# A chunked recurrence with full-array chunk steps in a written order on the tensor engine, and its triangular solve taken half a sequence at a time

## The chip, the cores and the metric

The kernel runs on one core of a Trainium2 chip. The metric is the device time of one execution in microseconds (us); lower is better. A core has a tensor engine (PE, with its weight loads shown apart as PEld), a vector engine (DVE), a scalar engine (ACT), GpSimd (POOL) and a sync engine (SP), which here issues the DMAs. Each engine runs its own instructions strictly in order, and waits for others by semaphores. TensorE has two clock levels, 1.2 and 2.4 GHz; a granted clock of 1.00 is the upper one.

## What is computed

One decoder block over 1024 tokens of width 1024: a combined projection, a gated unit (SGU) on half of the channels, a linear recurrence (RWKV7, 8 heads of 64 x 64 state) on the other half, an output projection, and cross-attention over 256 memory tokens. Everything is f32. Cut to the part that the change touches:

```python
def rwkv7_step(state, inp):
    r, w, k, v, a, bb = inp
    sa = jnp.einsum('bhvk,bhk->bhv', state, a)
    state = state * w[:, :, None, :] + sa[..., None] * bb[:, :, None, :] + v[..., None] * k[:, :, None, :]
    y = jnp.einsum('bhvk,bhk->bhv', state, r)
    return state, y
...
h  = x + W_out [ SGU_group(z_A) ; RWKV7_group(z_B) ],   z = RMSNorm(x) @ W_in
h  = h + MemXAttn(RMSNorm(h), RMSNorm(mem))
```

## The kernel before

**Big products.** A projection is made of "dense" products, 128x512 outputs with 128x128 weights. For f32 accuracy each is three fp32r products of high and low parts: `mm3` (L174 to L176). They carry most of the work, and in the recurrence they are interleaved with it so that TensorE has something to do while a chunk's chain runs through other engines.

**The recurrence.** Heads go in 4 pairs, a pair's 1024 tokens in 2 halves of 512 (8 halves in all), a half in 2 quarters, a quarter in 4 chunks of 64 tokens. For each half:

- `elementwise` (first product at L558) makes decays and the scaled operands `ra` (r and a) and `bk` (b and k).
- `grams` (L631) makes the chunks' inner products, masks them on DVE (L636, L638, L639, L641), writes the 16x16 diagonal blocks to DRAM (L640), reads them back with one block per partition (L647), inverts them there in 14 dependent steps on DVE (L648, then L652 and L654 in turn), writes the inverses (L655) and reads them back as `t16` (four DMAs, L659).
- `turn` (L670, L676) transposes v and bk on TensorE.
- `solve` extends the 16x16 inverses to 64x64, in groups of 8 small products (L690), each waiting for DVE's or ACT's work on the one before; the first group reads `t16`.
- `serial` is the chain over chunks. In each, both heads of the pair are done by small products side by side in the array (64x64 or 128x64 parts of it): `us0` = state times a (L751), DVE adds it to `akv` (L752), `us1` = the solve's matrix `tt` times that (L754), ACT and DVE each copy one head to `avt` (L756, L757), `us2` = bk times avt (L760), DVE makes the new state (L764), and ACT copies it into a block-diagonal 128x128 tile `stdiag` (L767, five of them in turn). Every two chunks `outputs` forms y from `stdiag` (L731) and `avt` (L735), and ACT copies it out (L737).
- `finish` normalises y on DVE and ACT and writes it to DRAM.

**The order.** The loop at the end runs over 19 quarter steps. In each, `weave` interleaves the generators of several pipeline stages (serial of this quarter, solve of the next, grams one half ahead, elementwise further ahead) with 16 dense units of a projection tile (`z_fill`), or later with `out_proj`. A scheduler then still moves instructions within an engine's order; `behind` ties each solve group to the last `us1`. Stretches named here by "first chunk product" are cut at a half's first L754.

## Time and profile before

| | |
|---|---|
| time, median of 3 runs | 966.76 us (965.78 to 968.97) |
| the profiled execution | 965.16 us, its span 963.3 us |
| busy in the span | PE 936.3 us (97%), PEld 723.7 us (75%), DVE 576.1 us (60%), ACT 410.2 us (43%), POOL 50.2 us (5%) |
| recurrence region on PE | 248.67 us (first L558) to 697.37 us (first product of the next stage) |

Busy shares of TensorE count a product from its issue to its modelled end; products overlap in the pipeline, so the step from one start to the next is what a product takes of the engine. All times below are from the span's start.

### The profile page before, as it was taken

To read this page: it belongs to the slowest core of one execution; us is meant where nothing else is said; L and a number is where in the kernel's file an instruction comes from. 1 tells how busy PE (TensorE), PEld (TensorE's weight loads), DVE (VectorE), ACT (ScalarE), POOL (GpSimd) and SP (SyncE) were. 2 spreads that over 40 slices of the span, in tenths; PEclk is the share of its full clock that TensorE was granted. 3 is DMA by queue.
4 is the path that set the end of the run, shared out by engine and by line. 5 is a ranking of instruction groups with operands and counts; after the bars stand their busy time and mean duration, and the time that the engine had idled before them with its cause. 6 is when DMAs were issued, how large, how long until landed. Compare 5 with 4: busy or idle time off the path is not lost.

```text
span 963.3 us, 17125 instructions
## 1 busy us (share of the span) xinstructions
PE 936.3 (97%) x6724; PEld 723.7 (75%) x6724; DVE 576.1 (60%) x1343; ACT 410.2 (43%) x918; POOL 50.2 (5%) x110
## 2 busy tenths in 40 slices
PE   6999999999999999999999999999999999999997
PEld 5978888888776667666666666666788778888885
DVE  5867234344575786767676787765677654444333
ACT  6764122224433545353535372534356643333222
POOL 0001000010100000000000000000000000000000
PEclk9999999999999999999999999999999999999999
DMA  8762011122112111111111172333472300000011
GB/s 316 252 224 97 12 69 67 66 95 81 40 49 48 34 30 38 38 45 37 48 37 48 37 242 80 99 92 97 130 248 70 127 23 1 22 22 22 22 43 46
DMA packets 86097, 76.93 MB, mean 80 GB/s; under 512 B 38272, under 2 KB 58752, under 8 KB 86016
## 3 DMA queue, kind: packets, MB, share of 16 engines
q1 hardware_dynamic: 84864, 73.73, 24.6%
q10 hardware_dynamic: 1152, 2.10, 0.6%
q8 instruction: 53, 0.87, 0.4%
q14 instruction: 28, 0.23, 0.1%
HBM read 62.17 MB, written 13.64 MB: 79 GB/s over the span
## 4 chain that ended last, share of the span: by engine, by line
PE 86%; DVE 5%; DMA 3%; issue 2%; ACT 2%; POOL 1%; SPq 0%; POOLq 0%; DVEq 0%; ACTq 0%
PE mm L174 23%; PE mm L175 22%; PE mm L176 21%; PE cb L690 5%; PE us L754 2%; PE yps L731 2%; PE us L760 2%; PE us L751 1%; PE co L631 1%; PE yps L735 1%; PE co L676 1%; DMA xr<-in_xT 1%; DMA w_raw<-in_w_sv 1%; DMA pr<-in_w_qT 1%; PE co L429 1%
## 5 line engine op out<-in xcount | busy, mean ns | idle before, releaser
L174 PE MATMUL mm<-xh,w_hi 128*128 128x512 f32 x400 | 167.3, 418 | 0.0
L175 PE MATMUL mm<-xl,w_hi 128*128 128x512 f32 x400 | 161.0, 402 | 0.0
L176 PE MATMUL mm<-xh,w_lo 128*128 128x512 f32 x400 | 159.9, 400 | 0.0
L154 DVE TENSOR_TENSOR w_lo<-w_raw,w_hi 128x512 fp32r<-128x512 f32 x115 | 78.7, 686 | 65.7 <-ACT w_hi L153 63.4
L153 ACT CAST w_hi<-w_raw 128x512 fp32r<-128x512 f32 x115 | 71.1, 619 | 97.8 <-PE mm L175 89.9
L174 PEld LDWEIGHTS mm<-xh,w_hi 128*128 128x128 f32 x400 | 75.3, 188 | 18.6 <-issue 2.4
L176 PEld LDWEIGHTS mm<-xh,w_lo 128*128 128x128 f32 x400 | 75.1, 188 | 15.5 <-issue 0.8
L175 PEld LDWEIGHTS mm<-xl,w_hi 128*128 128x128 f32 x400 | 75.2, 188 | 15.0 <-issue 2.1
L174 PE MATMUL mm<-wo,w_hi 128*128 128x512 f32 x128 | 53.4, 417 | 0.2 <-DVE kp_l L921 0.2
L175 PE MATMUL mm<-wo,w_hi 128*128 128x512 f32 x128 | 53.1, 415 | 0.0
L176 PE MATMUL mm<-wo,w_lo 128*128 128x512 f32 x128 | 52.8, 413 | 0.1
L174 PE MATMUL mm<-vp_h,p_hi 128*128 128x512 f32 x128 | 51.3, 401 | 0.0
L767 ACT COPY stdiag<-state 64x64 f32<-64x64 f32 x120 | 29.1, 243 | 50.3 <-DVE state L764 42.0
L174 PE MATMUL mm<-kp_h,w_hi 128*128 128x512 f32 x128 | 50.1, 391 | 0.0
L176 PE MATMUL mm<-kp_h,w_lo 128*128 128x512 f32 x128 | 50.0, 391 | 0.0
L176 PE MATMUL mm<-vp_h,p_lo 128*128 128x512 f32 x128 | 50.0, 390 | 0.0
L175 PE MATMUL mm<-vp_l,p_hi 128*128 128x512 f32 x128 | 49.9, 390 | 0.0
L175 PE MATMUL mm<-kp_l,w_hi 128*128 128x512 f32 x128 | 49.9, 390 | 0.0
L989 DVE TENSOR_REDUCE mx<-mm 128x2 f32<-128x512 f32 x16 | 11.1, 691 | 41.7 <-PE mm L176 41.7
L495 ACT ACTIVATE t<-mm,vec 128x512 f32<-128x512 f32 x34 | 23.3, 684 | 21.5 <-PE mm L176 21.4
L756 ACT COPY avt<-us 64x64 f32<-64x64 f32 x64 | 13.1, 205 | 44.7 <-PE us L754 44.1
L757 DVE COPY avt<-us 64x64 f32<-64x64 f32 x64 | 14.5, 226 | 29.0 <-ACT avt L756 27.5
(271 smaller groups left out, 2068.0 us busy)
## 6 DMA issues: line engine op xcount, KB each, us to landing
w_raw<-in_w_blk SPq DMA_DIRECT2D x50, 256.0 KB, 2.7
w_raw<-y_scr SPq DMA_DIRECT2D x32, 256.0 KB, 3.0
w_raw<-in_w_kv SPq DMA_DIRECT2D x17, 256.0 KB, 4.0
xr<-in_xT SPq DMA_DIRECT2D x8, 512.0 KB, 5.7
w_raw<-in_w_out SPq DMA_DIRECT2D x16, 256.0 KB, 2.6
h_all<-in_x SPq DMA_DIRECT2D x16, 256.0 KB, 4.2
pr<-in_w_qT SPq DMA_DIRECT2D x8, 512.0 KB, 4.2
w_raw<-in_w_o SPq DMA_DIRECT2D x16, 256.0 KB, 2.7
```

The lines of the kernel that those rows point to most:

```text
L153: nc.scalar.copy(out=hi, in_=src)
L154: (eng or nc.vector).tensor_tensor(out=lo, in0=src, in1=hi.bitcast(F32), op=ALU.subtract)
L174: nc.tensor.matmul(ps, lh, rh, start=first, stop=False)
L175: nc.tensor.matmul(ps, lh, rl, start=False, stop=False)
L176: nc.tensor.matmul(ps, ll, rh, start=False, stop=last)
L495: nc.scalar.activation(out=t1[:, 1:HT + 1], in_=ps, func=AF.Copy, scale=vc("mu", b))
L690: nc.tensor.matmul(ps[R[hh], c, :], fl(hh, c), fr(hh, c), start=True, stop=True)
L731: nc.tensor.matmul(yps[R[j], 0:P], ra[:, c0 + c - 1 + j, 0, :], st_d[(i - 1 + j) % NST], start=True, stop=False, skip_group_check=True)
L754: mm = nc.tensor.matmul(us[R[hh], 1, :], tt[R[hh], c, :], akv[R[hh], c, :], start=True, stop=True)
L757: nc.vector.tensor_copy(out=avt[0:64, c, R[1]], in_=us[R[1], 1, :])
L760: nc.tensor.matmul(us[R[hh], 2, :], bkt[:, c, R[hh]], avt[:, c, R[hh]], start=True, stop=True)
L767: D_COPY(nc)(out=st_d[(i + 1) % NST][R[hh], R[hh]], in_=s_new[R[hh]])
```

## The change

The chunk step is done with three products over the full 128x128 array: `us0` (now L755) multiplies r and a at once with the block-diagonal state, so that its upper half is already the state's part of y, and two DVE additions (L757) put its lower half into a second block-diagonal tile `abdiag`, while ACT copies the y part out (L759); `us1` is L765 with one ACT copy to `avt` (L766); `us2` is L769, from which two DVE operations (L775) write the block-diagonal state itself. So the state's copies (L767) and L731 fall away. The other part of y (L787) is made once in a quarter and added on DVE (L789). `us` has one PSUM tile for its three parts. The solve takes a half at a time, four waits in place of five per quarter, 16 products to a group (L708; the third makes two groups at once), so `t16` is one tile whose four DMAs (L675) all belong to the first group. The loop runs over 10 steps of a half with 32 dense units in a full one (`z_stream`, which fetches its next weights ahead), and TensorE's order is the order of the program, with no scheduler (`manual_schedule`). The stages of a half keep their distance: grams and solve one half ahead of serial, elementwise two. The projection tile that stood third before the loop is now the first one in it.

```diff
 LOGA = math.exp(-0.5)
 SHIFT = 19.4
 W_RAW = 3
-NST = 5
-Y_LAG = 2
 QC = 4
 NRA = 3
-W_G = (0.0, 0.4)
-W_T = (0.263, 0.465)
-N_T16 = 3
-W_E = (0.2, 0.964)
-W_S = (0.337, 0.95)
-G3 = 10
-N_PROJ = 11
+W_Y1 = (0.0, 0.03)
+W_G = (0.01, 0.18)
+W_T0 = (0.28, 0.40)
+W_Y0 = (0.55, 0.57)
+W_T1 = (0.58, 0.68)
+W_S = (0.64, 1.0)
+W_E = (0.30, 0.98)
+W_F = (0.08, 0.36)
 W_C = (0.0, 1.0)
-W_F = (0, 0.836)
-N_END = 1
-D_COPY = lambda nc: nc.scalar.copy
+N_PROJ = (14, 28, 28)
 W_HL = 3
 N_KV = (11, 14)
-AF_S = True
-AF_Y = False
...
-        st_t = [rw.tile([P, C], F32, name=f"state{i}") for i in range(2)]
-        st_d = [rw.tile([P, P], F32, name=f"stdiag{i}") for i in range(NST)]
-        for t in st_d:
+        st_d = [rw.tile([P, P], F32, name=f"stdiag{i}") for i in range(2)]
+        ab_d = [rw.tile([P, P], F32, name=f"abdiag{i}") for i in range(2)]
+        for t in st_d + ab_d:
...
+        def z_stream(blocks, then):
+
+            num = lambda pw: 9 + 4 * pw[0] + pw[1]
+            nxt = load_blk(w_blk[num(blocks[0])])
+            for n, pw in enumerate(blocks):
+                cur, nxt, raws = nxt, [], []
+                for h in range(2):
+                    ps = mm_ps()
+                    ts = slice(h * HT, (h + 1) * HT)
+                    for kk in range(KT):
+                        hi, lo = cur[kk // 4]
+                        mm3(ps, hi[:, kk % 4, :], lo[:, kk % 4, :], xh[kk][:, ts], xl[kk][:, ts], kk == 0, kk == 7)
+                        i = 8 * h + kk
+                        if n + 1 < len(blocks):
+                            if i in (1, 2):
+                                raws.append(fetch(w_blk[num(blocks[n + 1])][:, 4 * i - 4:4 * i, :], [P, 4, P]))
+                            if i in (8, 12):
+                                nxt.append(halves(raws[len(nxt)], [P, 4, P]))
+                        elif i == 12:
+                            next(then)
+                        if kk < 7:
+                            yield
+                    z_evac(*pw)(h, ps)
+                    yield
...
-        def behind(on):
-
-            return tc.issue_after(state["last"]) if on and state["last"] is not None else nullcontext()
...
+            u["t16"] = t16 = rw.tile([P, NC, C], F32, name="t16")
             for j in range(2):
-                quarters[2 * i + j]["t16"] = t16 = rw.tile([P, QC, C], F32, name="t16", bufs=N_T16)
                 for hh in range(2):
-                    nc.sync.dma_start(out=t16[R[hh]], in_=ti[j, hh, :, 0:C, :].rearrange("c s t -> s c t"))
+                    nc.sync.dma_start(out=t16[R[hh], QC * j:QC * j + QC, :],
+                                      in_=ti[j, hh, :, 0:C, :].rearrange("c s t -> s c t"))
             yield
 
...
+        def solve(i):
+
+            u, qs = halves_u[i], quarters[2 * i:2 * i + 2]
+            t16 = u["t16"]
+            of = lambda key, hh, c, rows: qs[c // QC][key][hh][rows, c % QC, :]
+
+            def pair_mm(ps, fl, fr):
+                ps = ps.rearrange("p (c t) -> p c t", c=NC)
+                for c in range(NC):
+                    for hh in range(2):
+                        nc.tensor.matmul(ps[R[hh], c, :], fl(hh, c), fr(hh, c), start=True, stop=True)
                 return ps
 
...
+            ps = pair_mm(cb_ps(), lambda hh, c: of("ntl", hh, c, R[hh]), lambda hh, c: t16[R[hh], c, :])
...
+            pa = pair_mm(co_ps(), lambda hh, c: of("akl", hh, c, R[1]), lambda hh, c: qs[c // QC]["avt"][R[1], c % QC, R[hh]])
...
+        def serial(i):
+
+            u = halves_u[i]
+            ra, dc, tt, akv = u["ra"], u["dc"], u["tt"], u["akv"]
+            u["y"] = ytok = rw.tile([P, 4, P], F32, name="ytok", bufs=2)
+            for c in range(NC):
+                q = quarters[2 * i + c // QC]
+                avt, bkt, cq = q["avt"], q["bkt"], c % QC
+                first = i % 2 == 0 and c == 0
+                last = i % 2 == 1 and c == NC - 1
+                n = state["i"]
+                state["i"] += 1
+                dcc = dc[:, c:c + 1]
+                s_old, s_new, ab = st_d[n % 2], st_d[(n + 1) % 2], ab_d[n % 2]
+                us = psC.tile([P, 3, P], F32, name="us")
+                yc = ytok[R[c % 2], c // 2, :]
+                if first:
+                    nc.gpsimd.memset(yc, 0.0)
+                    for hh in range(2):
+                        nc.vector.tensor_copy(out=ab[R[hh], R[hh]], in_=akv[R[hh], c, :])
+                else:
+
+                    nc.tensor.matmul(us[:, 0, :], ra[:, c, :, :], s_old, start=True, stop=True)
+                    for hh in range(2):
+                        nc.vector.tensor_tensor(out=ab[R[hh], R[hh]], in0=us[R[1], 0, R[hh]], in1=akv[R[hh], c, :],
+                                                op=ALU.add)
+                    nc.scalar.copy(out=yc, in_=us[R[0], 0, :])
+                    if not last:
+                        sd = rw.tile([P, P], F32, name="sd")
+                        nc.scalar.activation(out=sd, in_=s_old, func=AF.Copy, scale=dcc)
+                yield
+
+                nc.tensor.matmul(us[:, 1, :], tt[:, c - c % 2:c - c % 2 + 2, :], ab, start=True, stop=True)
+                nc.scalar.copy(out=avt[R[0], cq, :], in_=us[R[c % 2], 1, :])
+                yield
+                if not last:
+                    nc.tensor.matmul(us[:, 2, :], bkt[:, cq, :], avt[:, cq, :], start=True, stop=True)
+                    for h2 in R:
+                        if first:
+                            nc.vector.tensor_scalar(out=s_new[h2, h2], in0=us[h2, 2, h2], scalar1=dcc[h2],
+                                                    scalar2=None, op0=ALU.mult)
+                        else:
+                            nc.vector.scalar_tensor_tensor(out=s_new[h2, h2], in0=us[h2, 2, h2], scalar=dcc[h2],
+                                                           in1=sd[h2, h2], op0=ALU.mult, op1=ALU.add)
+                yield
+
+        def outputs(n):
...
+            gr, avt = q["gr"], q["avt"]
+            yps = psC.tile([P, 512], F32, name="yps")
             for c in range(QC):
                 for hh in range(2):
+                    o = P * (c // 2) + 64 * hh
+                    nc.tensor.matmul(yps[R[c % 2], o:o + 64], gr[:, c, hh, :], avt[:, c, R[hh]], start=True, stop=True)
+            yt = u["y"][:, 2 * (n % 2):2 * (n % 2) + 2, :]
+            nc.vector.tensor_tensor(out=yt, in0=yt, in1=yps[:, 0:256].rearrange("p (c v) -> p c v", c=2), op=ALU.add)
...
+        for w in range(2):
+            z_block(9 + w, z_evac(0, w))
         proj = out_proj(steps_0, ahead)
-        for n in range(-3, NQ):
-            ok = lambda m: 0 <= m < NQ
-            e_now = ok(n + 3) and (n + 3) % 2 == 0
-            streams = [(grams((n + 2) // 2) if ok(n + 2) and n % 2 == 0 else iter(()), 5, *W_G),
-                       (turn(n + 2) if ok(n + 2) else iter(()), 2, *W_T),
-                       (elementwise(halves_u[(n + 3) // 2]) if e_now else iter(()), 7, *W_E),
-                       (solve(n + 1) if ok(n + 1) else iter(()), 5, *W_S),
-                       (serial(n) if ok(n) else iter(()), 5, *W_C),
-                       (finish(halves_u[n // 2 - 1]) if n > 0 and n % 2 == 0 else iter(()), 3, *W_F)]
-            if n in fills:
-                fill = z_fill(*fills[n])
-                weave(streams + [(fill, 16, 0.0, 1.0)])
+        blocks = [(0, 2), (1, 0), (1, 1), (1, 2), (0, 3), (2, 0), (2, 1), (2, 2), (1, 3), (3, 0), (3, 1), (3, 2), (2, 3), (3, 3)]
+        dense = chain(z_stream(blocks, proj), proj)
+        NH = 2 * NPAIR
+        none = iter(())
+        n_dense = {-2: 16, 5: 16 + N_PROJ[0], 6: N_PROJ[1], 7: N_PROJ[2]}
+        with tc.manual_schedule(engines={mybir.EngineType.PE}):
+            for n in range(-2, NH):
+                ok = lambda m: 0 <= m < NH
+                streams = [(outputs(2 * n - 1) if ok(n - 1) else none, 1, *W_Y1),
+                           (grams(n + 1) if ok(n + 1) else none, 5, *W_G),
+                           (serial(n) if ok(n) else none, 3 * NC, *W_C),
+                           (turn(2 * n + 2) if ok(n + 1) else none, 2, *W_T0),
+                           (outputs(2 * n) if ok(n) else none, 1, *W_Y0),
+                           (turn(2 * n + 3) if ok(n + 1) else none, 2, *W_T1),
+                           (elementwise(halves_u[n + 2]) if ok(n + 2) else none, 7, *W_E),
+                           (solve(n + 1) if ok(n + 1) else none, 4, *W_S),
+                           (finish(halves_u[n - 1]) if ok(n - 1) else none, 3, *W_F)]
+                weave(streams + [(dense, n_dense.get(n, 32), 0.0, 1.0)])
                 for st in streams:
                     drain(st[0])
-                drain(fill)
-            else:
-                weave(streams + [(proj if n > G3 else iter(()), N_PROJ, 0.0, 1.0)])
-                for st in streams:
-                    drain(st[0])
-        weave([(finish(halves_u[-1]), 3, 0.0, 0.6), (proj, N_END, 0.0, 1.0)])
-        drain(proj)
+            weave([(outputs(2 * NH - 1), 1, 0.0, 0.0), (finish(halves_u[-1]), 3, 0.1, 0.5), (dense, 8, 0.0, 1.0)])
+        drain(dense)
 
 
     with tc.tile_pool(name="tail", bufs=1) as tl:
```

**TensorE at a half's start, before.** The grams (L631) of the next half among dense products (`mm`), with `us1` (L754) and `us2` (L760) of the half's first chunk.

```order
L176 MATMUL mm<-xh_99,w_lo 128x512
L631 MATMUL co<-ra,bk 64x128 x16
L174 MATMUL mm<-xh_100,w_hi 128x512
L175 MATMUL mm<-xl_108,w_hi 128x512
L176 MATMUL mm<-xh_100,w_lo 128x512
L754 MATMUL us<-akv,tt 64x64 x2
...
L174 MATMUL mm<-xh_102,w_hi 128x512
L631 MATMUL co<-ra,bk 64x128
L760 MATMUL us<-avt,bkt 64x64 x2
L631 MATMUL co<-ra,bk 64x128 x15
```

The scheduler put `us1` one dense triple behind the first 16 gram products, and `us2` inside the second 16.

**The same place after** (L169 to L171 are the dense products, L647 the grams, L765, L769 and L755 the three steps of the chain).

```order
L647 MATMUL co<-ra,bk 64x128 x16
L169 MATMUL mm<-xh_100,w_hi 128x512
L170 MATMUL mm<-xl_108,w_hi 128x512
L171 MATMUL mm<-xh_100,w_lo 128x512
L765 MATMUL us<-abdiag_1926,tt 128x128
...
L647 MATMUL co<-ra,bk 64x128 x16
L769 MATMUL us<-avt,bkt 128x128
L169 MATMUL mm<-xh_102,w_hi 128x512
...
L755 MATMUL us<-stdiag_1925,ra 128x128
```

The second 16 gram products and the chain's steps now stand at fixed places, one dense triple apart; `us2` and the next `us0` come behind the second 16 grams.

**DVE at that place, before**: the masks of the grams (L636 to L641) and what is between them.

```order
L636 TENSOR_TENSOR an<-co,cst 128x256
L638 TENSOR_TENSOR nt_3947<-co,cst 64x256
L639 TENSOR_TENSOR ak_3948<-co,cst 64x256
L641 TENSOR_TENSOR gr<-co,cst 128x4x64
L757 COPY avt<-us 64x64
L641 TENSOR_TENSOR gr<-co,cst 128x4x64
L793 TENSOR_TENSOR ytok<-ytok,grs 128x512
L762 TENSOR_SCALAR state_1925<-us,dc 128x64
```

The rows of `finish` (gsm, gsv, L793) and the state update (L762) lie ahead of the masks or between those of the two quarters.

**DVE there after**: the masks are L652 to L657, the state update is L775, `finish` L797 to L803, the gate L494 and L500.

```order
L500 SCALAR_TENSOR_TENSOR zg<-gth,zg 128x512
L797 TENSOR_REDUCE gsm<-ytok 128x8
L654 TENSOR_TENSOR nt_4467<-co,cst 64x256
L655 TENSOR_TENSOR ak_4468<-co,cst 64x256
L657 TENSOR_TENSOR gr<-co,cst 128x4x64
L652 TENSOR_TENSOR an<-co,cst 128x256
L657 TENSOR_TENSOR gr<-co,cst 128x4x64
L798 SCALAR_TENSOR_TENSOR ytok<-gsm,ytok 128x512
L803 TENSOR_REDUCE gsv<-ysq 128x8
...
L775 SCALAR_TENSOR_TENSOR stdiag_1925<-us,dc,sd 64x64 x2
```

The gate, the sum of `finish` and the chain's additions are queued ahead of the first mask, L798 and L803 stand between the two quarters' masks, and the state update behind nearly all of them.

## Rows read from the trace of the kernel before

**Rows 1.** Windows, dense products alone: stretch; us, busy PE, PEld, DVE, ACT, clock.

```profile
248.67:305.61 56.94, 40.01 (x152) 26.98 (x151) 4.74 (x7) 4.80 (x7) 1.00 0.19 52
305.61:544.48 238.87, 137.65 (x439) 74.61 (x438) 13.85 (x19) 12.29 (x18) 1.00 0.15 39
544.48:697.37 152.89, 98.79 (x324) 56.01 (x324) 18.21 (x25) 1.38 (x2) 1.00 0.40 117
```

**Rows 2.** The chain of work that ended last, share of the span by engine.

```profile
PE 86%; DVE 5%; DMA 3%; issue 2%; ACT 2%; POOL 1%; SPq 0%; POOLq 0%; DVEq 0%; ACTq 0%
```

**Rows 3.** Timeline of PE in dense work: start, duration; first and last of 46.

```profile
139.69 0.39 PE L174 MATMUL mm<-xh,w_hi 128*128 128x512 f32 x1
...
149.88 0.39 PE L174 MATMUL mm<-xh,w_hi 128*128 128x512 f32 x1
```

**Rows 4.** Timeline of PE in the recurrence.

```profile
399.17 0.40 PE L176 MATMUL mm<-xh,w_lo 128*128 128x512 f32 x1
399.40 0.60 PE L676 MATMUL co<-cst,bk 128*128 128x128 f32 x4
399.75 0.48 PE L174 MATMUL mm<-xh,w_hi 128*128 128x512 f32 x1
400.07 0.39 PE L175 MATMUL mm<-xl,w_hi 128*128 128x512 f32 x1
400.30 0.40 PE L176 MATMUL mm<-xh,w_lo 128*128 128x512 f32 x1
400.62 0.33 PE L751 MATMUL us<-state,ra 64*64 64x64 f32 x4
400.88 0.50 PE L174 MATMUL mm<-xh,w_hi 128*128 128x512 f32 x1
401.22 0.40 PE L175 MATMUL mm<-xl,w_hi 128*128 128x512 f32 x1
```

**Rows 5.** Groups on PE, region: xcount (two passes each) | busy, mean ns | idle before.

```profile
L754 PE MATMUL us<-akv,tt 64*64 64x64 f32 x256 | 21.9, 242 | 0.6
L751 PE MATMUL us<-state,ra 64*64 64x64 f32 x240 | 21.0, 239 | 2.1 <-DVE state L764 2.1
L760 PE MATMUL us<-avt,bkt 128*64 128x64 f32 x240 | 20.5, 245 | 1.0 <-DVE avt L757 0.7
```

**Rows 6.** Timeline of PE: first grams of the program, first solve products of two halves.

```profile
263.55 1.09 PE L631 MATMUL co<-ra,bk 64*64 64x128 f32 x16
...
296.79 0.33 PE L690 MATMUL cb<-t,an 64*64 64x64 f32 x2 [0.96 <-DMA t<-t_img]
...
422.98 0.33 PE L690 MATMUL cb<-t,an 64*64 64x64 f32 x2
```

**Rows 7.** Timeline of DVE, same half: a mask, then the inversion's start and end.

```profile
395.24 0.42 DVE L638 TENSOR_TENSOR nt<-co,cst 64x256 f32<-64x256 f32 x1
...
402.20 0.57 DVE L648 TENSOR_TENSOR nt<-ak,cst 64x256 f32<-64x256 f32 x1
...
415.56 0.16 DVE L654 TENSOR_TENSOR nt<-nt,xtmp 64x14 f32<-64x14 f32 x1
```

**Rows 8.** Timeline of SP, same half: the inversion's DMAs as issued.

```profile
398.14 0.59 SPq L647 DMA_DIRECT2D ak<-nt_scr  x1
...
415.75 0.58 SPq L655 DMA_DIRECT2D t_img<-nt  x1
418.64 2.58 SPq L659 DMA_DIRECT2D t<-t_img  x4
```

**Rows 9.** All work of the region, windows: us, busy of PE, PEld, DVE, ACT, POOL.

```profile
248.67:697.37 448.70, 439.92 (x4153) 304.51 (x4152) 319.48 (x890) 202.36 (x520) 23.74 (x54) 1.00 0.24 67
```

**Rows 10.** Groups on DVE and ACT in the region.

```profile
L752 DVE TENSOR_TENSOR akv<-akv,us 128x64 f32<-128x64 f32 x60 | 12.6, 211 | 16.7 <-PE us L751 15.7 <-ACT akv L709 0.7 <-ACT ytok L737 0.2
L764 DVE SCALAR_TENSOR_TENSOR state<-us,dc,sd 128x64 f32<-128x64 f32 x56 | 15.9, 283 | 18.5 <-PE us L760 17.4 <-PE yps L735 0.4
L784 DVE SCALAR_TENSOR_TENSOR ytok<-gsm,ytok 128x512 f32<-128x512 f32 x8 | 5.4, 677 | 0.1
```

More of the change, by code (lines that the diff above doesn't have):

```diff
@@ L538, in tile_hybrid_block @@
         R = (slice(0, 64), slice(64, 128))
-        state = {"i": 0, "last": None}
-        def behind(on):
-            return tc.issue_after(state["last"]) if on and state["last"] is not None else nullcontext()
+        state = {"i": 0}
         def elementwise(u):
             p, h = u["p"], u["h"]
-            r, k, v = u["r"], u["k"], u["v"]
+            r, k = u["r"], u["k"]
             ts = slice(h * HT, (h + 1) * HT)
@@ L679, in turn @@
             yield
[L681 to L696 removed]
+        def solve(i):
[7 more added lines that the diff above has]
+                        nc.tensor.matmul(ps[R[hh], c, :], fl(hh, c), fr(hh, c), start=True, stop=True)
+                return ps
+            tt = rw.tile([P, NC, C], F32, name="tt", bufs=2)
+            z = rw.tile([P, NC, C], F32, name="zz")
+            akv = rw.tile([P, NC, C], F32, name="akv", bufs=2)
+            mk = lambda m: cs_(m).unsqueeze(1).broadcast_to([P, NC, C])
             nc.vector.transpose(out=flat(tt), in_=flat(t16))
[L698 removed]
+            ps = pair_mm(cb_ps(), lambda hh, c: of("ntl", hh, c, R[hh]), lambda hh, c: t16[R[hh], c, :])
             nc.vector.tensor_tensor(out=z, in0=ps, in1=mk("m16"), op=ALU.mult)
             yield
[L701 removed]
+            ps = pair_mm(cb_ps(), lambda hh, c: tt[R[hh], c, :], lambda hh, c: z[R[hh], c, :])
             nc.vector.tensor_tensor(out=t16, in0=t16, in1=ps, op=ALU.add)
@@ L822, in y_load @@
                 return load_split(y_scr[4 * g:4 * g + 4, :, ts].rearrange("k p t -> p k t"), [P, 4, P])
+            if not h_all:
+                for k in range(4):
+                    wo_part(0, k)
             nxt = y_load(steps[0][0], steps[0][2])
             if not h_all:
+                yield
                 h_all.extend(big.tile([P, T], F32, name="h_all", tag=f"big0{i}") for i in range(8))
-                for k in range(4):
-                    wo_part(0, k)
             for n, (g, nh, i) in enumerate(steps):
```

109 lines of the change are left out of this document (14 added, 95 removed).

## The prediction, made before the changed kernel ran

> **What bounds the kernel now.** I read the chain of work that ended last first: 86% of the span is TensorE's [rows 2]. The change lies in the recurrence region, 448.70 us of the 963.3 [rows 9]; I cut it at the halves' first chunk products into a start of 56.94 us, five steady halves of 238.87 and a late part of 152.89 [rows 1]. Next I want what a dense product takes of TensorE: 46 of them start from 139.69 to 149.88, so 45 steps of 0.2264 us [rows 3]. By the written order the three stretches hold 159, 458 and 327 products of this size (944, with 32 of elementwise); the windows show about as many records [rows 1]. That is 36.0, 103.7 and 74.0 us. The remaining 235 us of the region are small products, what it costs to go to them and back, and waits. So the question has two sides: how much content the change takes from TensorE, and how much waiting the fixed order puts in.
>
> **The price of a small step.** In the timeline [rows 4], 399.17 to 400.07 holds two dense products and four full-array transposes of 128 columns: 0.90 - 0.45 = 0.45, so 0.11 for a pass of 128 columns. From 400.30 to 401.22 two dense products and one packed step (L751, two heads, two passes of 64 columns) take 0.92, so the step adds 0.47. The two heads run side by side, so its content is two passes of 64 columns, 0.11; the other 0.36 I put to two changes of the array's shape, 0.18 each. A full-array f32 step, two passes of 128 columns and no change, should cost 0.22.
>
> The Trainium skill, TensorEngine Tiling (Array Packing), section Theoretical Speedup, gives packing of dimensions up to 64 a speedup of up to 2x, which speaks against the change. By it alone the 184 steps would cost 0.11 us more each, some 20 us. For a step that stands alone among dense products the rows above say the opposite, 0.47 against 0.22.
>
> **What TensorE is spared.** Counted in the two orders over the region, changes of shape fall from 563 to 144. Of the 563, 73 are between two packed shapes; no row shows these alone, so they lie between nothing and 0.18, and I take half. That makes (490 - 144) x 0.18 + 73 x 0.09 = 69 us. Products removed: 184 packed pairs (240, 256 and 240 records, four to a pair [rows 5]) at 0.11, 20.2 us, and 60 of L731 (128 columns in pairs), 6.6. Added: 184 full-array steps at 0.22, 40.5, and eight transposes, 0.9. Net -69 - 27 + 41 = **-54 us**. The solve's products stay as many and as large. The 30 dense products that the region gains stood ahead of it before; all dense work is priced at 0.2264 on both sides and drops out. The DMAs are as many.
>
> **What TensorE waits for instead.** Before, a scheduler put ready work in front of waiting work, and the steps of the chain idled only 2.1, 0.6 and 1.0 us in the whole region [rows 5]. Now everything behind a waiting product waits as well. I price the new order's content with the numbers above and put it against what must arrive, stretch by stretch.
>
> *Start.* From the first L558 (248.67) to the first gram (263.55) before took 14.9 us [rows 6]; the new content there is only 10.1 us, and the elementwise chain through DVE, ACT and POOL is the same, so 14.9 stays. From the first gram to the first solve product (296.79) took 33.2, and that one still waited 0.96 for t16 [rows 6]; the new order holds 21.4 us of content there, so about 12 us are idle. From there to the first chunk product is 16.8 of content and about 0.4 of returns. Sum 65.3 with 140 dense; before, without the 19 dense more, 56.94 - 4.3 = 52.6. So **+12.7**. Bounds: +6, if the inversion is quicker with an emptier DVE; +16, if each solve group also waits almost a microsecond for DVE.
>
> *Steady halves.* From first us1 to the next the order holds 42.8 us of content, 22.6 of it dense. From the first gram (zero) the first solve product is 25.9 of content away. On DVE the last mask that the inversion needs stands behind the gate, two sums and a subtraction of finish at 0.68 each (L784) [rows 10] and seven masks at 0.42 [rows 7], after grams of about 1.1 [rows 6]: it ends near 7. From that mask's end (395.66) to the first solve product before took 27.3 us [rows 6 to 8]: a write and a read (L647 issued at 398.14), the inversion from 402.20 to 415.72, a write (415.75) and four reads (from 418.64 on). Some of it was DVE and SP work of other stages in between; the new DVE order has less there, and I take 2.4 off. So t16 is complete near 32, and as the first group needs all four reads, TensorE stands **6 us** behind its content. An earlier wait is inside these 6: the next us0 needs a state update that is queued on DVE behind almost all masks, near 8.5 against 5.6 of content. The next half's chunk products follow on the solve, so each half pays again, unlike a delay that is caught up. A half is 48.8, five are 244; before, with 42 more dense, 238.87 + 9.5 = 248.4. So **-4.4**. Bounds: 1 us of wait (t16 ready when TensorE comes) gives -29; 10 us (the whole 27.3, and the DVE queue on top) gives +16.
>
> *Late part.* DVE's mean operation is 319.48/890 = 0.36 us [rows 9]. In half 5 the order has 136 of them between the chain's starts, 49 us, against 41.3 of content: 52 with waits. Half 6: 35.6 and the t16 wait and some returns, 46. Half 7 has 28 dense products for eight chunks, little over one for each of 24 steps: 0.26 us of cover for a return through DVE or ACT of 0.21 to 0.28 [rows 10] and the ways there and back, so some 0.4 each stay open: 43.5 + 10. Sum 151.5 against 152.89 + 7 x 0.2264 = 154.5: **-3**. Bounds -15 and +15.
>
> Together 12.7 - 4.4 - 3 = +5.3 us on the profiled 965.16, or 970.5; the median of the runs is 1.6 above that execution, so **972 us**.
>
> **The rivals.**
>
> *A, the waits are hidden, faster.* If t16 comes when TensorE reaches the solve, a half is 43.8; with +6 at the start, -29 in the halves and -8 late it is -31, **936 us**. For it: on the trace the solve's first product of the later half (422.98) shows no idle time before it [rows 6]. Against: there the scheduler chose when to start it. It decides where the way from mask to t16 drops from 25 to about 20 us.
>
> *B, no change.* The waits eat just the 54 us: **964 to 970**. For it only that the sums nearly cancel.
>
> *C, DVE sets the pace, slower.* The chain's additions and state updates come in two halves of 64x64 now and outputs get an addition; by count a half has 105 to 136 operations, 38 to 49 us at 0.36. If the small ones cost more than L752's 0.21 or queue behind the gate at the wrong time, halves become 53: +21 more there and +6 late, **999 us**. Against: DVE was busy 319 of 449 us [rows 9].
>
> *D, shape changes are not what costs.* If the 0.36 belongs to any short product among dense ones, the full-array steps cost 0.47 too, and what is spared shrinks by 46: **985 to 1000** as part hides in the waits. Against: the four transposes show no such addition [rows 4]. That packing pays, as the page has it, would end here too.
>
> **How the numbers follow.** The measurement can tell about 0.3%, 2.9 us, from no change. Chances: my forecast 0.47 (own range 964 to 984), A 0.33 (930 to 957), B 0.10, C 0.07, D 0.03. From these faster 0.37, same 0.13, slower 0.50. The range reaches down past A's middle to 934, which leaves about 0.14 below, and up to 994, which leaves about 0.06 above.
>
> **What would show it.** Right: no L751-like packed steps, a full-array step adding 0.22 between dense products; the region's content down by some 54 us; idle time of TensorE ahead of the first solve group (L708), released by t16's DMAs, about 12 us in the start and 3 to 6 in each half; idle ahead of L755 released by L775. Wrong: no idle there (A), or idle ahead of L755 and L765 released by DVE in most chunks (C), or full-array steps adding more than 0.3 (D), or a granted clock under 1.00 in the start.

## The result, and the profile after

The changed kernel takes **1003.4 us** (median of 4, 1000.8 to 1005.1) against 966.3 before, a ratio of 1.0376 with a 95% interval of 1.0346 to 1.0405. Slower was forecast, but at 972 us, in a range that ended at 994: the sign held, the size and the range did not. The profiled execution has a span of 1001.6 us, 38.3 more than before.

First the profile page's chain of work that ended last, as [rows 2]; then the windows of all work in the region, as [rows 9]; then those of the dense products by stretch, as [rows 1].

```profile
PE 67%; DVE 18%; DMA 5%; issue 4%; ACT 3%; POOL 1%; SPq 1%; POOLq 0%; ACTq 0%; DVEq 0%
```

```profile
242.63:733.21 490.58, 414.66 (x3703) 318.70 (x3702) 352.88 (x927) 189.48 (x423) 22.03 (x59) 0.96 0.23 64
```

```profile
242.63:309.62 66.99, 38.57 (x133) 25.66 (x132) 4.45 (x6) 4.09 (x6) 0.87 0.12 31
309.62:564.60 254.98, 146.67 (x481) 80.60 (x480) 15.01 (x20) 13.79 (x20) 0.99 0.15 39
564.60:733.21 168.61, 99.48 (x331) 59.90 (x331) 18.30 (x25) 1.38 (x2) 0.94 0.40 115
```

TensorE's share of the chain falls from 86% to 67% and DVE's rises from 5% to 18%: the engine with the work now waits for the one without. In the region TensorE is busy 415 of 491 us, before 440 of 449. The granted clock, 1.00 in all three stretches before, is 0.87 in the start and 0.94 in the late part. With dense products priced as in the prediction, the stretches stand so:

| stretch | before, same dense work | after | change | forecast |
|---|---|---|---|---|
| start | 52.6 | 67.0 | +14.4 | +12.7 |
| five steady halves | 248.4 | 255.0 | +6.6 | -4.4 |
| late part | 154.5 | 168.6 | +14.1 | -3 |
| outside the region | | | +3.2 | 0 |

The chain of waits on TensorE, whole execution (us in total, times, longest):

```profile
PE us L765 <- ACT ytok L759: 22.9, 30, 2.5
PE cb L708 <- DMA t<-t_img: 17.3, 7, 7.8
PE us L755 <- DVE stdiag L775: 11.1, 11, 2.0
PE mm L169 <- ACT w_hi L148: 9.7, 3, 6.4
PE us L755 <- DVE stdiag L772: 9.2, 4, 3.4
PE co L647 <- DVE gr L657: 6.3, 12, 1.0
```

Before, the three steps of the chain idled 3.7 us in the region [rows 5]; now us1 and us0 (L765, L755) idle 43, and the solve (L708) 17. The largest wait, us1's, stood in the prediction's walk nowhere by name. The price of a step is as forecast. In this timeline of TensorE, after, a full-array step (L769) stands between dense products:

```profile
470.81 0.40 PE L171 MATMUL mm<-xh,w_lo 128*128 128x512 f32 x1
471.05 0.38 PE L769 MATMUL us<-avt,bkt 128*128 128x128 f32 x2
471.19 0.48 PE L169 MATMUL mm<-xh,w_hi 128*128 128x512 f32 x1
471.50 0.39 PE L170 MATMUL mm<-xl,w_hi 128*128 128x512 f32 x1
```

From 470.81 to 471.50 are two dense products and the step, 0.69 - 0.45 = 0.24 us, forecast 0.22; the packed step added 0.47 [rows 4]. Over 64 full-array steps that stand so without a wait the medians are 0.23 to 0.24, over 51 packed ones of the kernel before 0.47. The first grams of this half start at 459.91, and what follows on DVE is the queue of the prediction:

```profile
461.65 0.68 DVE L797 TENSOR_REDUCE gsm<-ytok 128x8 f32<-128x512 f32 x1
462.36 0.42 DVE L654 TENSOR_TENSOR nt<-co,cst 64x256 f32<-64x256 f32 x1
...
465.63 0.69 DVE L803 TENSOR_REDUCE gsv<-ysq 128x8 f32<-128x512 f32 x1 [0.70 <-ACT ysq L801]
466.24 0.41 DVE L652 TENSOR_TENSOR an<-co,cst 128x256 f32<-128x256 f32 x1
466.68 0.42 DVE L654 TENSOR_TENSOR nt<-co,cst 64x256 f32<-64x256 f32 x1
...
467.91 0.57 DVE L775 SCALAR_TENSOR_TENSOR stdiag<-us,dc,sd 64x64 f32<-64x64 f32 x2
```

The last mask that the inversion needs ends at 467.1, 7.2 us in (forecast near 7). On TensorE, us0 then starts at 468.63, 8.7 us in (forecast near 8.5), and the solve at 492.65, 32.7 us in (forecast near 32):

```profile
468.63 0.46 PE L755 MATMUL us<-stdiag,ra 128*128 128x128 f32 x2 [1.34 <-DVE stdiag L775]
...
492.65 0.27 PE L708 MATMUL cb<-t,an 64*64 64x64 f32 x1
```

So the three times were near, yet the solve's first product has no idle time before it here: TensorE itself came only then. In the five steady halves it starts 31.5 to 34.8 us after the first gram, and this is what TensorE waits for in them:

```profile
PE us L765 <- ACT ytok L759: 17.0, 19, 2.5
PE us L755 <- DVE stdiag L772: 5.8, 3, 2.6
PE co L647 <- DVE gr L657: 4.5, 9, 1.0
PE us L755 <- DVE stdiag L775: 2.7, 2, 1.3
PE cb L708 <- DMA t<-t_img: 0.7, 1, 0.7
```

Together these are 30.7 us, 6.1 in a half, which is the size of the 6 us that were forecast; but the forecast had them at the solve's t16, and only 0.7 stand there. What held TensorE in the half above lies before the solve, at the next chunk's us0 and us1, on DVE and ACT:

```profile
472.66 0.38 PE L755 MATMUL us<-stdiag,ra 128*128 128x128 f32 x2
...
473.30 0.75 DVE L494 SCALAR_TENSOR_TENSOR zr<-mm,der,t 128x512 f32<-128x512 f32 x1 [1.25 <-ACT t L490]
473.97 0.56 DVE L664 TENSOR_TENSOR nt<-ak,cst 64x256 f32<-64x256 f32 x1
...
474.56 0.23 DVE L757 TENSOR_TENSOR abdiag<-us,akv 64x64 f32<-64x64 f32 x1
474.71 0.16 DVE L668 TENSOR_TENSOR xtmp<-ak,nt 64x14 f32<-64x14 f32 x1
474.90 0.23 DVE L757 TENSOR_TENSOR abdiag<-us,akv 64x64 f32<-64x64 f32 x1
...
475.16 0.26 ACT L759 COPY ytok<-us 64x128 f32<-64x128 f32 x1 [0.41 <-DVE abdiag L757]
...
475.47 0.49 PE L765 MATMUL us<-abdiag,tt 128*128 128x128 f32 x2 [1.50 <-ACT ytok L759]
```

us0 is issued at 472.66 and us1 2.81 us later. The additions stand in DVE's queue behind a projection's evacuation (L494, itself waiting for ACT) and the inversion's first step; then ACT's y copy waits for them, and us1 for the copy. us1 uses nothing that the copy reads; it only shares the PSUM tile `us` with it, and to that I put the wait (e1 below bears it out). The Trainium skill, PSUM — Partial Sum Buffer, section "PSUM bank collisions raise a hardware error", asks for semaphores that keep engines apart by bank and quadrant of 32 partitions; the rows agree for us1, which writes all 128 partitions of the tile and starts at 475.47, when the copy (475.16 + 0.26) has ended. That the copy waits for the additions is not asked for there, since they read partitions 64 to 127 of the tile and the copy 0 to 63.

### The profile page after: what moved, and what is told of

It reads as the page before. It is cut to its first block, busy times and chain, and to the rows that moved or that the text cites. A ratio compares the mean times of both kernels' runs of the same rounds, so it can differ in the third digit from the quotient of the medians.

```text
span 1001.6 us, 16186 instructions
## 1 busy us (share of the span) xinstructions
PE 905.2 (90%) x6236; PEld 732.4 (73%) x6236; DVE 606.6 (61%) x1375; ACT 394.8 (39%) x818; POOL 48.1 (5%) x113
## 4 chain that ended last, share of the span: by engine, by line
PE 67%; DVE 18%; DMA 5%; issue 4%; ACT 3%; POOL 1%; SPq 1%; POOLq 0%; ACTq 0%; DVEq 0%
PE mm L169 19%; PE mm L170 18%; PE mm L171 18%; PE cb L708 3%; DVE stdiag L775 2%; DVE nt L670 2%; DVE xtmp L668 1%; DMA t_img<-nt 1%; DMA t<-t_img 1%; PE us L765 1%; DVE w_lo L149 1%; DVE abdiag L757 1%; DVE gr L657 1%; DMA w_raw<-in_w_sv 1%; POOL grs L145 1%
## 5 line engine op out<-in xcount | busy, mean ns | idle before, releaser
L169 PE MATMUL mm<-xh,w_hi 128*128 128x512 f32 x400 | 174.8, 437 | 0.0
L171 PE MATMUL mm<-xh,w_lo 128*128 128x512 f32 x400 | 158.2, 395 | 0.0
L170 PE MATMUL mm<-xl,w_hi 128*128 128x512 f32 x400 | 158.1, 395 | 0.0
L171 PEld LDWEIGHTS mm<-xh,w_lo 128*128 128x128 f32 x400 | 76.1, 190 | 16.9
L169 PEld LDWEIGHTS mm<-xh,w_hi 128*128 128x128 f32 x400 | 76.5, 191 | 12.8 <-issue 2.1
L169 PE MATMUL mm<-wo,w_hi 128*128 128x512 f32 x128 | 58.2, 455 | 0.9 <-DVE kp_l L931 0.9
L170 PE MATMUL mm<-wo,w_hi 128*128 128x512 f32 x128 | 52.1, 407 | 0.0
L171 PE MATMUL mm<-wo,w_lo 128*128 128x512 f32 x128 | 52.0, 406 | 0.0
L765 PE MATMUL us<-abdiag,tt 128*128 128x128 f32 x128 | 30.6, 322 | 23.0 <-ACT ytok L759 22.9
L169 PE MATMUL mm<-vp_h,p_hi 128*128 128x512 f32 x128 | 51.3, 401 | 0.0
L765 PEld LDWEIGHTS us<-abdiag,tt 128*128 128x128 f32 x128 | 21.1, 195 | 41.3 <-ACT ytok L759 38.4
L171 PE MATMUL mm<-kp_h,w_lo 128*128 128x512 f32 x128 | 50.1, 392 | 0.0
L169 PE MATMUL mm<-kp_h,w_hi 128*128 128x512 f32 x128 | 50.0, 391 | 0.0
L171 PE MATMUL mm<-vp_h,p_lo 128*128 128x512 f32 x128 | 50.0, 390 | 0.0
L762 ACT ACTIVATE sd<-stdiag,dc 128x128 f32<-128x128 f32 x56 | 22.4, 400 | 57.1 <-DVE stdiag L775 38.4
L755 PEld LDWEIGHTS us<-stdiag,ra 128*128 128x128 f32 x120 | 20.9, 190 | 32.5 <-issue 20.2
L755 PE MATMUL us<-stdiag,ra 128*128 128x128 f32 x120 | 24.9, 290 | 20.6 <-DVE stdiag L775 11.1
```

The lines of the kernel that those rows point to most:

```text
L169: nc.tensor.matmul(ps, lh, rh, start=first, stop=False)
L170: nc.tensor.matmul(ps, lh, rl, start=False, stop=False)
L171: nc.tensor.matmul(ps, ll, rh, start=False, stop=last)
L755: nc.tensor.matmul(us[:, 0, :], ra[:, c, :, :], s_old, start=True, stop=True)
L762: nc.scalar.activation(out=sd, in_=s_old, func=AF.Copy, scale=dcc)
L765: nc.tensor.matmul(us[:, 1, :], tt[:, c - c % 2:c - c % 2 + 2, :], ab, start=True, stop=True)
```

## The experiments

Theory L is the prediction's: the loop of grams, inversion and solve sets the half, and what is saved elsewhere comes back as a wait for t16. Theory R: the return of each chunk step is a loss of its own. Theory C: the clock's falls are the loss (this is not the prediction's rival C). Theory F: the fixed order is, since a waiting product holds back ready ones.

### One wait at a time (e1, e2, e3)

e1 moves ACT's y copy behind its copy to avt:

```diff
-                    nc.scalar.copy(out=yc, in_=us[R[0], 0, :])
...
                 nc.scalar.copy(out=avt[R[0], cq, :], in_=us[R[c % 2], 1, :])
+                if not first:
+                    nc.scalar.copy(out=yc, in_=us[R[0], 0, :])
```

> ACT's copy of the y part (L759) is issued behind its copy to avt (L766), so us1 (L765) waits for DVE's two additions alone; nothing else changes. Theory R (the return of the chain step): us1's idle time, 23.0 us in the changed kernel with ACT's y copy as its releaser, goes to under 8 us, and the time falls by about as much: 983 us, between 977 and 988. Theory L (the loop of grams, inversion and solve, the prediction's own): in the halves the first solve product comes within 1 us of t16's landing, so what is saved ahead of it comes back as a wait for t16, and only what is saved behind it counts: idle time before L708 rises from 17 to about 27 us and the time is 993 us, between 989 and 998. Theory C (the tensor clock's falls are most of the loss): no change beyond what the waits give; the falls at 283 to 297 and after 595 stay.

Measured 1004.8 us (1002.9 to 1005.8): nothing gained. The chain of waits of this kernel:

```profile
PE cb L708 <- DMA t<-t_img: 23.5, 18, 7.9
PE us L764 <- DVE abdiag L757: 11.1, 14, 1.6
PE us L755 <- DVE stdiag L776: 10.9, 10, 2.0
PE us L755 <- DVE stdiag L773: 9.3, 4, 3.4
```

us1's wait halves (22.9 to 11.1), and 6.2 us come back at the solve, as theory L has it: in the steady halves us1's wait falls from 17.0 to 9.5 and the solve's rises from 0.7 to 7.0. More comes back at us2 (L770 here), which uses nothing of the y part either and now waits for the late copy. The wait stands mostly at its weight loads, so the list above does not have it; the view of L770 names the copy (us, times):

```profile
  ACT ytok L767: 11.3, 36
```

From the start of the dense product before a us2 to that of the product behind it are 0.53 us in the mean of 43 places, 0.41 in 45 of the changed kernel: some 7 us over the 60 chunks. The granted clock is lower too, 0.98 against 0.99 in the steady halves and 0.93 against 0.94 late. That all came back neither theory forecast: R alone falls, and L's 989 to 998 is missed as well.

e2 reads t16 early from an image of zeros, e3 does both:

```diff
+            for j in range(2):
+                for hh in range(2):
+                    nc.sync.dma_start(out=t16[R[hh], QC * j:QC * j + QC, :],
+                                      in_=t_fix[j, hh, :, 0:C, :].rearrange("c s t -> s c t"))
             nc.sync.dma_start(out=L, in_=diag(ns))
```

> The four reads of t16 are issued ahead of the inversion and come from an image in DRAM that only holds zeros, so the solve doesn't wait for the inversion; all other work stays, the inversion's result being left unused. Theory L: the 17.4 us of idle time before L708 vanish and the halves shorten a little (DVE and the chain are then the limit); start 67 to about 56 us, late part 8 us less, together 983 us, between 977 and 988. Theory R: the chain waits stay at 23 us before L765 and 21 us before L755, and rise where PE comes to them earlier, so 985 to 992. Theory C: with the idle stretches at 283 to 297, 597 to 605 and 651 to 659 the clock's falls vanish too; of some 24 us of granted clock lost in the changed kernel about 14 lie there, so 975 us or less.

> Both edits: y copy late, and t16 read early from an image of zeros (the inversion's result unused). Theory L: what the y copy's move saves ahead of the solve is no longer taken back, so the two together save more than the sum of each alone, 25 to 30 us beyond the early t16: about 955 us. Theory R: each wait counts by itself, and the two together save the sum of both, about 962 us. If DVE is the bound behind these (106 to 120 operations a half, 39 us busy of 50), neither shortens the halves: 975 or more.

e2 takes 981.2 us (978.7 to 985.1), where L had put it; it is below R's range and above C's. e3 takes 968.1 (963.5 to 970.2), between R's 962 and the 975 of a bound by DVE; L's 955 is missed. In e2 the start falls from 67.0 to 54.7 and the late part from 168.6 to 160.4, but the five steady halves stay at 255.5: there only 0.7 us had been waited for t16. Only with both edits do they fall, to 247.4. So the y copy is worth nothing alone and 13 us once t16 is out of the way, 8 of them in the steady halves: two limits of about the same length lie over each other there.

### The clock (e5)

e5 puts 36 unused dense products ahead of the first half's solve:

```diff
+            if i == 0:
+                fp = mm_ps()
+                for f in range(12):
+                    mm3(fp, xh[f % 8][:, 0:P], xl[f % 8][:, 0:P], xh[f % 8][:, 0:HT], xl[f % 8][:, 0:HT], f == 0, f == 11)
```

> 36 more dense products (12 units of projection with a result that nobody uses, 8.2 us of content) stand in TensorE's order ahead of the first solve group of the first half, where the changed kernel idles 7.8 us for t16 and its granted clock is then 0.50 from about 283 to 297. Theory C (the clock's falls follow the idle stretches and cost content): they lie in the idle time, the clock stays at 1.00, the solve and the dense work behind it go at full speed, and the start falls from 67.0 to 62 to 64 us: 999 us. If the clock has no part in it: 1003 within 2 us. If t16's wait is set by something that the products disturb: up to 1011.

Measured 999.0 us (997.9 to 1001.3), as theory C had it; the start is 64.3, just above its 62 to 64. In e1 and e10, which leave the start as it is, it is 66.9 and 67.0. In the changed kernel the wait for t16 is followed by dense products 0.43 apart in place of 0.23:

```profile
288.80 0.47 PE L708 MATMUL cb<-t,an 64*64 64x64 f32 x2 [7.76 <-DMA t<-t_img]
...
294.03 0.63 PE L170 MATMUL mm<-xl,w_hi 128*128 128x512 f32 x1
294.46 0.63 PE L171 MATMUL mm<-xh,w_lo 128*128 128x512 f32 x1
```

The window of the changed kernel over this stretch, its clock third from the end:

```profile
283.00:297.00 14.00, 7.50 (x55) 5.68 (x56) 2.89 (x8) 0.91 (x2) 0.31 (x2) 0.51 0.13 25
```

The same window of e5:

```profile
283.00:297.00 14.00, 13.29 (x118) 10.23 (x117) 3.77 (x7) 1.87 (x3) 0.37 (x2) 1.00 0.13 25
```

So 8 us more work made the start 2.7 us shorter, with the clock at its upper level in this window: C holds there. Behind the region e5 is another 2.7 us shorter (258.8 against 261.5), where the changed kernel's clock fell once more (0.93 from 775 to 800) and which e5 does not touch; so of the 4.4 us only the start's part is shown to come from the filling. The other falls, after the solves' waits of the late part above all, were not tried one by one. The mean clock of 0.96 in the region's 490.58 us leaves some 20 us as the most that the lower level can have taken there directly.

### The order (e4, e7, e6)

e4 leaves TensorE's order to the scheduler, e7 does so with e1's y copy; e6 gives the kernel before the order of its program:

```diff
-        with tc.manual_schedule(engines={mybir.EngineType.PE}):
+        if True:
```

> The changed kernel with TensorE's order left to the scheduler as before, the rest the same. Theory F (the fixed order is the loss, since a waiting product holds back ready ones): the full-array steps' 54 us of spared content show, 940 to 960 us. Theory R or L: the waits are of dependences (one PSUM tile for us, four reads for one t16, half as many and longer groups), and the scheduler can only move them: 985 to 1005 us.

> The changed kernel with TensorE's order left to the scheduler and ACT's y copy behind its copy to avt. With a free order us1 idles 6.1 us, 4.8 of it for that copy: Theory R gives 949 to 951 us; Theory L, that what is saved there comes back elsewhere, 954 within 2 us.

> The kernel before, its TensorE order in the recurrence taken from the program in place of the scheduler; packed steps, five stdiag tiles and the solve by quarters stay. Theory F: the fixed order costs whatever the steps are; content by the prices of the prediction even falls (395 changes of shape in place of 563), waits take over: 990 to 1015 us. If the loss belongs to the new steps and the solve of a half (one us tile, four reads for one t16): 955 to 975 us.

e4 takes 954.3 us (952.6 to 957.0), in F's range and 0.9868 of the kernel before (0.9847 to 0.9889); e7 **951.1** (950.0 to 951.7), 0.9844 (0.983 to 0.9859), the best of all. e6 takes 1105.8 (1101.5 to 1111.1): slower, as F has it, but 90 us above F's range; its mean clock in the region is 0.88, which F had not priced. In the chain of waits of e7 little is left of us1's and the solve's:

```profile
PE us L764 <- DVE abdiag L757: 2.4, 7, 0.6
...
PE cb L708 <- DMA t<-t_img: 2.3, 3, 1.0
```

The y copy, worth nothing in the fixed order, is worth 3.2 us here, as R had it, though that is near what two medians can tell apart. The windows of the region, e1 (fixed order) and then e7, which differ by the edit above alone, with the clock third from the end:

```profile
243.78:737.94 494.16, 423.80 (x3703) 322.21 (x3702) 353.68 (x927) 185.41 (x423) 21.78 (x59) 0.95 0.23 64
243.60:682.38 438.78, 419.96 (x3707) 313.80 (x3706) 349.22 (x925) 184.35 (x421) 23.32 (x59) 1.00 0.25 68
```

So F holds, in this form: with the scheduler the waits go, and the clock stays at its upper level. One rival was not parted from it. The edit names TensorE alone, but the scheduler orders DVE and ACT otherwise too: of DVE's 925 operations in e7's region at least 254 stand elsewhere than in e1. How much of the gain is TensorE's own order and how much the queues that serve it is not shown.

### The steps (e10, e11)

Both put packed steps back into the changed kernel, e10 in the fixed order, e11 in a free one; the core of the edit:

```diff
-                    nc.tensor.matmul(us[:, 0, :], ra[:, c, :, :], s_old, start=True, stop=True)
+                    for x in (1, 0):
+                        for hh in range(2):
+                            nc.tensor.matmul(us[R[hh], 0, R[x]], ra[R[hh], c, x, :], s_old[R[hh], R[hh]],
+                                             start=True, stop=True)
```

> The changed kernel with the steps' products packed again (64x64 or 128x64 for each head, r apart from a; one addition and two state updates on DVE, a copy to avt each on ACT and DVE, two y copies on ACT behind them), in the fixed order of the program; solve, outputs and weave stay. By the prediction's prices TensorE's content in the region rises from 383 to 425 us. If spared content counts in the fixed order: 1030 to 1047 us. If the waits hide it: 1005 within 8 us.

> The same packed steps with the order left to the scheduler, to be set against 951.1 us of the full-array steps with a late y copy in a free order. Content in the region by the prices: 443 against 397 us. If the full-array steps are worth their content once the order is free: 985 to 997 us. If the chain's returns set the pace there and not the content: 950 to 965 us.

Measured 1047.2 us (1041.2 to 1050.0) and 988.7 (986.0 to 991.4). With the kernels that differ from them in the steps or the order alone:

| | fixed order | free order | the order costs |
|---|---|---|---|
| packed steps | 1047.2 (e10) | 988.7 (e11) | 58.5 |
| full-array steps | 1004.8 (e1) | 951.1 (e7) | 53.7 |
| the steps save | 42.4 | 37.6 | |

Both times lie in the range or at the edge of the range for spared content that counts. The two effects add up to within 5 us. The steps' saving was priced at 42 and 46 us ahead of these runs, and is 0.20 to 0.23 us for each of 184 steps; it contains what the edit changes on DVE and ACT (a copy to `avt` on each, one more y copy). The Trainium skill, TensorEngine Tiling (Array Packing), section Theoretical Speedup, gives packing a speedup of up to 2x; here it goes the other way, packed steps costing 38 to 42 us more. That the cost is the way out of the full array's shape and back is the prediction's reading of 0.47 us against 0.24 for a step among dense products; no run parts it from the step itself.

### What else holds the fixed order up (e8, e9, e12 to e15)

e8 makes us0 of e3 read a tile that stays zero; e9 adds a second `us` tile, at the cost of one of the dense products' three PSUM tiles:

```diff
-                s_old, s_new, ab = st_d[n % 2], st_d[(n + 1) % 2], ab_d[n % 2]
+                s_old, s_new, ab = st_d[0], st_d[1], ab_d[n % 2]
...
-    psA = ctx.enter_context(tc.tile_pool(name="psA", bufs=3, space=PSUM))
+    psA = ctx.enter_context(tc.tile_pool(name="psA", bufs=2, space=PSUM))
...
-                us = psC.tile([P, 3, P], F32, name="us")
+                us = psC.tile([P, 3, P], F32, name="us", bufs=2)
```

> TensorE's fixed order with three waits taken away: t16 early from an image of zeros, the y copy late, and us0 multiplying by a state tile that stays zero, so that no chunk waits for the one before (all instructions stay, the state update writes a tile that no product reads). The content of the region at the prediction's prices is 383 us. If these prices hold, what is left is the start's 10 us, some 11 us before us1 and 6 before the grams: a region of 410 to 420 us and a time of 920 to 930. If the prices are too low and the full-array steps do not spare 54 us: 940 or more.

> The kernel without waits as before (t16 early from zeros, y copy late, us0 on a state tile that stays zero), and now with two us tiles in PSUM in turn, for which the dense products have two tiles in place of three. In the one with a single us tile, us0 still idled 20.8 us behind L777, the DVE operation that reads the old us tile, so its edit did not take that wait away. If this wait and what hangs on it is a loss of its own: its idle time goes, the region falls from 456 to about 433, and the time is 940 to 950. Theory L (what is saved comes back at the next wait): us1's waits for the additions rise in its place, 958 or more.

e8 takes 967.8 us, as e3: us0 must still wait until DVE has read the old `us` tile, so the edit did not remove its wait, and the run says nothing of the content's price. e9 takes 986.0; the 18 us more than e8 lie outside the recurrence, whose region is 455.8 against 456.2. us1's wait in e9, 11.3 us in e3:

```profile
PE us L765 <- DVE abdiag L758: 29.2, 24, 3.7
```

us0's 20.8 us are gone and 18 came back at us1, as theory L had it: the additions stand in the same queue of DVE as the state update did. e12 does the same to the free order of e7.

> Full-array steps, y copy late, free order, and two us tiles in turn, for which the dense products have two PSUM tiles in place of three. us0 idled only 1.4 us in the free order, so a second tile can save little: 949 to 952 us. If a dense tile fewer holds up the dense products: 953 to 965 us.

Measured 972.1 us (970.7 to 975.5), above both ranges, region 438.5 against 438.8: a second `us` tile gives nothing, and two dense tiles in place of three cost 21 us, 17 of them behind the recurrence (277 against 260 from the region's end to the last product) and the rest ahead of it.

e13 and e14 take the inversion's steps out of DVE's queue in e3 and e9, e15 the token shift (L494) in e3:

```diff
-            for s in range(1, 15):
...
-            nc.vector.scalar_tensor_tensor(out=dst, in0=ps, scalar=d_mu[:, b:b + 1], in1=t1[:, 0:HT],
-                                           op0=ALU.mult, op1=ALU.add)
+            nc.scalar.activation(out=dst, in_=ps, func=AF.Copy, scale=vc("mu", b))
```

> The kernel with t16 early and the y copy late (968 us, region 459), with the 28 DVE operations of the inversion's 14 steps (L668, L670) left out in each half; its result was not used there. DVE loses 5.5 us of work in a half of 50. If DVE's queue sets when the chain's additions and state updates come, and so the pace of the halves: the waits before L755 and L765 (20.5 and 11.4 us) fall by half and the region by 20 to 35 us, 935 to 948 us. If the waits come from the chain itself (its products' and engines' own latencies): 962 to 968 us.

> The same, and us0 on a state tile that stays zero with two us tiles in turn (the kernel that took 986 us, 18 us of it outside the recurrence for the third PSUM tile of the dense products), again with the inversion's 28 operations left out. That one lost us0's wait of 20.8 us and got it back before us1, behind additions that stood in DVE's queue. If the queue is the cause: region 456 falls to 415 to 435, and the time to 945 to 965. If not: 980 to 986.

> The kernel with t16 early and the y copy late (968 us, region 459), in which the projection's tiles are written by one ACT operation straight from PSUM: the token shift, a DVE operation of 0.75 us that waits for ACT (L494), is left out (28 in the recurrence). In the changed kernel it stands in DVE's queue right ahead of the chain's additions in five of eight chunks of a steady half. If its place in that queue is what us1 waits for: the idle time before L765 (11.4 us) falls under 5, that before L755 somewhat, and the region from 459 to 435 to 447: 945 to 956 us. If the additions are late for other reasons: 962 to 968.

They take 963.6, 981.4 and 963.6 us; the region falls by 7 each time (459.4 to 451.9, 455.8 to 448.8, 459.4 to 452.2), well short of what a single culprit would give: all three times lie where they were put for the case that DVE's queue is not the cause. In e15 us1's wait falls from 11.4 to 6.0, near what was expected of L494's place, and us0's rises from 20.5 to 23.8. No one group of DVE's work that was taken out is the cause; that TensorE stops at the next wait instead is what e15's us0 and e9's us1 show. Such edits also let the scheduler move other work of DVE: of e3's operations that remain, at least 70 stand elsewhere in e13 and 141 in e15.

## Why the prediction was wrong

**What held.** The price of a step, and the count of changes of shape (563 and 144 stand in the traces). Of the 54 us forecast to be spared, the steps' part, priced 42 to 46, measured 38 to 42. In the steady halves the last mask, the next us0 and the first solve product come 7.3, 8.8 and 33.1 us after the first gram in the mean of five, walked as near 7, 8.5 and 32. That slower came out has the reason that was given, waiting products that hold back ready ones.

**What was luck.** The sign. The sum had its +5.3 from the start alone; the steady halves and the late part were forecast to gain 7.4 us and lost 20.7. The start's +14.4 for +12.7 is in part luck too: its wait for t16 is 7.8 us and not 12, and the way from there to the first chunk product takes 20.8 us and not 17.2, 8 of them at the lower clock.

**What failed.** The step "An earlier wait is inside these 6". The 6 us were put to t16 at the solve, the waits ahead of it were taken to vanish in them, and the waits of all other chunks to be nothing. The earlier waits are not inside that one, they are as long as it: TensorE comes to the solve when t16 does, and e2, which frees it of t16, gains nothing in the steady halves. A half came out at 51.0 us in place of 48.8, so 8.2 above its priced content of 42.8 in place of 6: 6.1 are the idle time above, and about 1.1 more lie in it unseen, since idle time counts from the modelled end of the product before, 0.39 - 0.2264 = 0.16 us late [rows 3], at each of the 34 waits; the last us is not accounted for. The walk named us0's one wait behind the masks (forecast 2.9 us a half; it is 0.6 to 2.6 in the five) but not us1's, which idles 22.9 us in all, because it followed DVE's queue to the masks and the state update, and for the other chunks looked at how long operations take and not at what stands ahead of them in DVE's and ACT's queues.

**The late part** was the larger miss, 17 of the 30 us that the region came out above the forecast. Halves 5, 6 and 7 took 55.3, 54.8 and 58.6 us, forecast 52, 46 and 53.5. Half 6 was given 35.6 + about 10 from its smaller content; but t16's arrival does not shrink with TensorE's content. The first solve product of that half comes 35 us after its first gram (618.0 to 653.1), against 22.1 of content. Behind such idle stretches the clock is at its lower level (0.57 from 597 to 605 and 0.62 from 650 to 659, mean 0.94 in the late part, so at most some 10 us of the 168.6), a cost that the sum had not at all and named only as a sign to look for. e5 shows it for the start; its share in the late part was not measured.

**The rivals.** A (waits hidden) fell, but e4 and e7 show it with a free order, where the waits on TensorE are few. Rival C (DVE sets the pace) comes nearest in time (999), and its second half, additions that queue behind the gate or its like, is what the trace shows at us1; DVE's total work is not the bound, since e13 and e15 took only 7 us from the region and 4 from the time. D, full-array steps at 0.47 us, fell with the 0.24 of the trace and with e10 and e11.

**What stays open.** How the remaining 17 us between e3 (968) and e7 (951) divide among the fixed order's waits, the clock and the other engines' orders. And e11 is 22 us slower than the kernel before: the half-long stages with packed steps are worse than the quarter-long ones, or its packed steps differ too much from the old ones (r apart, two state updates); this was not taken apart.

## What to carry to other kernels

A change can hold two opposite ones: price each by a kernel that does it alone. Here full-array steps save 38 to 42 us, and the written order, with the orders of the other engines that come with it, costs 54 to 58; the better kernel, 951 us, is the change without its order and with the y copy late. On an engine that issues in order, waits do not vanish in a later one unless that later one is longer than their sum; walk every wait to its arrival time through the queues of the engines that serve it, and where the chain has several limits of like length, expect nothing from removing one.

## What the runs showed that was not expected

The cost of a wait goes past its own length: with 7.8 us of idle time in the start TensorE's clock is 0.51 from 283 to 297, and 36 products whose result nobody uses made the start 2.7 us shorter. Moving a copy that one product waits for can hand its wait to the next product on the same PSUM tile, where a list of the engine's waits does not show it (us2 in e1). And the kernel before loses 140 us when its own program order is kept (e6), where us2 and us1 idle 61 and 38 us: its order was the scheduler's from the beginning, and at a mean clock of 0.88 in the region part of the loss is the clock's.
